# A hybrid decoder layer in TensorE's row: memory values in float32r, the norm of x placed earlier, eleven matmuls of ones ahead of the first product

## The chip, the core and the metric

The kernel runs on one core of one Trainium2 chip. The metric is the device time of one execution in microseconds (us), as a median over runs. A core has TensorE (PE in the profile, with its weight loads as PEld), VectorE (DVE), ScalarE (ACT), GpSimd (POOL) and SyncE (SP), which here only issues transfers. Each engine takes its instructions in the order in which they were written for it, and waits on semaphores for the others.

## The reference, cut to what matters

One decoder layer on x (1024 tokens of 1024 channels) with 256 memory tokens. The normalised input goes through one combined projection; three mixers use its columns (stick-breaking attention, an mLSTM, cross-attention to the memory tokens), their outputs are gated and merged, and a gated MLP with a short convolution follows. The change touches only the beginning, the norm of x and the keys and values of the memory:

```
h = _rmsnorm(x, g_mix[l])
(sb_q, sb_k, sb_v, ...) = jnp.split(h @ w_in[l], offsets, axis=-1)
...
y_xa = _memory_cross_attention(xa_q, _rmsnorm(mem, g_mem[l]), w_mem_kv[l], xa_g_q[l], xa_g_k[l])

def _memory_cross_attention(q, mem_n, w_kv, g_q, g_k):
    k, v = jnp.split(mem_n @ w_kv, 2, axis=-1)
```

## The kernel before, in words

Everything is stored transposed, channels on the 128 partitions and tokens along the free dimension, and x is handled in two halves of 512 tokens, half 1 first. A large product is made in float32r in three parts: an operand is split into a high piece (`hi`, an ACT copy that rounds to float32r) and a low piece (`lo`, a DVE subtraction of the high piece from the original), and `mm3` issues hi·hi, hi·lo and lo·hi into one PSUM bank. `split` (L135) and `wsplit` (L139) make these pieces. The memory's keys and values are the exception: `mem_mm` (L221) multiplies plain float32 tiles, one matmul per tile.

The first 60 us run like this. SP issues the vectors, the two halves of the memory (`y` tiles), the four key weights (`wk`), four pages of x's half 1, a small gate weight (`w_if`) and the four value weights (`wv`). ACT scales the memory by its gain (`mem_load`, L196). TensorE then makes the keys (`mem_mm` into the banks pk), 16 float32 matmuls of 128x512, and the values (into pv), another 16. Among them stand three small things: the norm factors of the memory (`mem_stats`: squares on ACT, adds on DVE, two matmuls with ones), those of x (`x_stats` and `rstd`: four squares on ACT, three adds on DVE, four matmuls with ones, a power on POOL), and `spread` (L172), which turns x's factors into rows by four DVE products with the identity and one matmul with ones. `x_norm` (L282) multiplies each of 8 channel tiles by gain and row factor on DVE (L287), and splits it into `h` tiles: hi on ACT, lo on DVE.

After the values comes the first projection, the queries and keys of the first attention pair (`chunks`, L389): two weights, `raw` tiles split into `whi` and `wlo`, times all 8 `h` tiles, 24 matmuls each, into two PSUM banks of the ring `pj`, which has two. `eq` and `ek` (L372 to L386) empty those banks with ACT copies and DVE subtractions. `gates_if` (L458) needs the first of them again for 16 matmuls, and `nat_chunks` (L348) the second. In that time the pages of x's half 0 arrive (L266), ACT squares them (L274), and the same norm is made for half 0.

Four things set the order around the change. The tiles of one tag are a ring with a fixed number of buffers (`raw`, `whi`, `wlo`: 2, `U`: 5, `pg`: 16), and the next user of a buffer waits until the last one is done. A scheduler places instructions by the order of the text and by priorities (`tc.high_priority`). Each engine then runs its row in that order. SP issues transfers in its own row too, so one that waits for a buffer holds back all behind it.

Of the kernel before, what the change touches and what calls it, by code (L numbers as in the profile page):

```python
# [11 lines left out]
F32R = mybir.dt.float32r  # L12
# [6 lines left out]
P = 128  # L19
D = 1024  # L20
S = 1024
HALF = 512
# [20 lines left out]
def tile_hybrid_layer(ctx: ExitStack, tc: tile.TileContext, xT, memT, vecs, w_t, w_n, w_kv, w_if,  # L43
# [58 lines left out]
    def hs(h):  # L102
        return slice(h * HALF, (h + 1) * HALF)
# [31 lines left out]
    def split(src, hi, lo, eng=None):  # L135
        nc.scalar.activation(hi, src, AF.Copy)  # L136
        (eng or nc.vector).tensor_sub(lo, src, hi.bitcast(F32))  # L137
# [48 lines left out]
    nc.scalar.activation(warm, nhalf[:, :1], AF.Square)  # L186
    mraw = []
    mg = [page() for _ in range(2)]

    def mem_load(j):  # L190
        t = T([P, S], "y")
        mraw.append(t)
        nc.sync.dma_start(t.rearrange("p (k m) -> p k m", k=4), memT[4 * j:4 * j + 4].rearrange("k p m -> p k m"))
        for i in range(4):
            c = slice(i * NMEM, (i + 1) * NMEM)
            nc.scalar.activation(mg[j][:, c], t[:, c], AF.Copy, scale=col(C_GMEM + 4 * j + i))  # L196

    mtags = itertools.cycle(("raw", "whi", "wlo"))

    def mem_w(which, b):  # L200
        t = T([P, S], next(mtags))
        nc.sync.dma_start(t, w_kv[which, b])
        return t

# [1 line left out]
    nc.vector.tensor_mul(gqk, col(C_GQ), col(C_GK))  # L206
    xkv_d = dtile([XAH, P, 2, NMEM], "xkv_d")

    def mem_stats():
        for t in mraw:  # L210
            nc.scalar.activation(t, t, AF.Square)
        a = mraw[0]
        nc.vector.tensor_add(a, a, mraw[1])
        for n in (512, 256):
            nc.vector.tensor_add(a[:, :n], a[:, :n], a[:, n:2 * n])
        pc = bank("tr")
        for t in range(2):
            nc.tensor.matmul(pc[:, t:t + 1], a[:, ts(t)], ones[:, :1], start=True, stop=True)
        return rstd_cols(pc[:, :2], 2, D)

    def mem_mm(pm, w, b):  # L221
        for m in range(2):
            for kk in range(2):
                k = 2 * b + kk
                c = slice((k % 4) * NMEM + m * P, (k % 4) * NMEM + (m + 1) * P)
                nc.tensor.matmul(pm[m], mg[k // 4][:, c], w[:, hs(kk)], start=(k == 0), stop=(k == KT - 1))  # L226

    def mem_keys(pm, rm):
        kns = []
# [62 lines left out]
    xp = {0: [], 1: []}  # L292
    wk, wv = [], []
    mem_load(0)
    wk.append(mem_w(0, 0))
    mem_load(1)
    for b in range(1, 4):
        wk.append(mem_w(0, b))
# [7 lines left out]
    for g in range(2):  # L306
# [1 line left out]
        hi = wif[:, :, 32 * g:32 * g + 4]  # L308
        nc.scalar.activation(hi, src, AF.Copy)
# [1100 lines left out]
```

## Time and profile before

| | |
|---|---|
| median of 3 runs | 1672.93 us (1672.88 to 1676.76) |
| the profiled execution's own time | 1674.48 us |
| its span in the trace | 1672.4 us |
| TensorE busy | 1645.0 us, 98% |
| DVE, ACT, POOL busy | 1209.2, 826.8, 52.8 us |
| first matmul starts | 6.91 us |
| first projection starts | 37.92 us |
| `gates_if` starts, `nat_chunks` starts | 49.96 us, 54.42 us |

A line of a timeline reads: start and length in us, engine, source line, operation, output and inputs, shape, count, and in square brackets the engine's idle time ahead of it with what ended it. Consecutive instructions of one kind are merged into a row with a count. TensorE's float32 matmul of 128x512 shows as two records, so a row of x8 is four matmuls. Records of matmuls overlap; what counts is the distance from one start to the next. SP's rows are issues, not transfers.

### The profile page before, as it was taken

What the parts mean: (1) busy time and instruction counts of PE and PEld (TensorE: products, weight loads), DVE (VectorE), ACT (ScalarE), POOL (GpSimd) and SP (SyncE); (2) the same over time, 40 slices, a digit from 0 to 9 for tenths busy, and PEclk for the clock granted to TensorE, in tenths of its full rate; (3) what the DMA queues carried; (4) which work ended last, traced back from release to release, by engine and by line L of the source; (5) the groups of instructions that cost most, each with busy time, mean ns of one, the idle gap of its engine ahead of it and who ended that gap; (6) DMA issues with size and microseconds to landing.
All of it is one profiled execution on the core that took longest, in us unless ns stands there. A gap on an engine that the chain in (4) does not pass through costs nothing.

```text
span 1672.4 us, 21192 instructions
## 1 busy us (share of the span) xinstructions
PE 1645.0 (98%) x7975; PEld 1338.0 (80%) x7975; DVE 1209.2 (72%) x1710; ACT 826.8 (49%) x1249; POOL 52.8 (3%) x95
## 2 busy tenths in 40 slices
PE   8999999999999999999999999999999999999999
PEld 4777777788877888888788888688888888788887
DVE  5648778777765666666557648997778877789864
ACT  4547667645555445556422334565455554543431
POOL 1000000010000001000000000000000000000000
PEclk9999999999999999999999999999999999999999
DMA  8410011234324555433755354222222221486131
GB/s 296 149 64 24 35 39 51 95 116 137 108 104 154 183 183 170 133 127 113 271 181 184 114 189 145 94 90 104 78 77 76 82 87 58 164 327 239 36 138 73
DMA packets 96249, 212.69 MB, mean 127 GB/s; under 512 B 12416, under 2 KB 36224, under 8 KB 96148
## 3 DMA queue, kind: packets, MB, share of 16 engines
q1 hardware_dynamic: 96148, 211.35, 37.1%
q8 instruction: 63, 1.03, 0.3%
q14 instruction: 38, 0.31, 0.1%
HBM read 156.71 MB, written 54.61 MB: 126 GB/s over the span
## 4 chain that ended last, share of the span: by engine, by line
PE 89%; DVE 4%; ACT 4%; DMA 3%; issue 1%; SPq 0%; POOLq 0%; POOL 0%; ACTq 0%; DVEq 0%
PE ps_pj L149 14%; PE ps_pj L150 14%; PE ps_pj L151 14%; PE ps_pv L150 6%; PE ps_pv L151 6%; PE ps_pv L149 6%; PE ps_tr L151 4%; PE ps_tr L149 4%; PE ps_tr L150 4%; PE ps_z L149 3%; PE ps_z L150 3%; PE ps_z L151 3%; PE ps_tr L434 2%; PE ps_pv L448 1%; PE ps_z L226 1%; PE ps_z L413 1%
## 5 line engine op out<-in xcount | busy, mean ns | idle before, releaser
L150 PE MATMUL ps_pj<-h,whi 128*128 128x512 f32 x620 | 242.2, 391 | 0.0
L136 ACT ACTIVATE whi<-raw 128x512 fp32r<-128x512 f32 (+1 forms) x112 | 93.6, 836 | 177.5 <-PE ps_pj L150 71.6
L149 PE MATMUL ps_pj<-h,whi 128*128 128x512 f32 x412 | 163.2, 396 | 0.9 <-DVE U L1053 0.9
L149 PE MATMUL ps_pj<-pg,whi 128*128 128x512 f32 x396 | 154.6, 390 | 0.0
L151 PE MATMUL ps_pj<-pg,wlo 128*128 128x512 f32 x380 | 148.0, 389 | 0.0
L150 PEld LDWEIGHTS ps_pj<-h,whi 128*128 128x128 f32 x620 | 116.5, 188 | 23.5 <-issue 0.2
L151 PE MATMUL ps_pj<-h,wlo 128*128 128x512 f32 x332 | 129.9, 391 | 0.1
L810 DVE SCALAR_TENSOR_TENSOR y<-U,vec,y 128x1023 f32<-128x1023 f32 x88 | 112.5, 1280 | 8.0 <-ACT y L808 8.0
L422 DVE TENSOR_TENSOR_SCAN U<-U 128x512 f32<-128x512 f32 (+3 forms) x96 | 88.6, 965 | 30.7 <-ACT U L415 29.8
L149 PEld LDWEIGHTS ps_pj<-h,whi 128*128 128x128 f32 x412 | 77.4, 188 | 18.3 <-issue 1.5
L137 DVE TENSOR_TENSOR wlo<-raw,whi 128x1024 fp32r<-128x1024 f32 x54 | 66.0, 1222 | 30.9 <-ACT whi L136 30.6
L149 PEld LDWEIGHTS ps_pj<-pg,whi 128*128 128x128 f32 x396 | 74.3, 188 | 15.8 <-DVE pg L1051 0.4
L151 PEld LDWEIGHTS ps_pj<-pg,wlo 128*128 128x128 f32 x380 | 71.3, 188 | 14.9 <-issue 0.2
L136 ACT ACTIVATE whi<-pg 128x512 fp32r<-128x512 f32 (+1 forms) x59 | 43.4, 738 | 72.2 <-PE ps_pv L150 20.7
L150 PE MATMUL ps_pj<-pg,whi 128*128 128x512 f32 x188 | 73.4, 390 | 0.0
L151 PEld LDWEIGHTS ps_pj<-h,wlo 128*128 128x128 f32 x332 | 62.3, 188 | 13.6 <-DVE wlo L137 0.6
L150 PE MATMUL ps_pv<-h,whi 128*128 128x512 f32 x164 | 63.8, 389 | 0.0
L808 ACT ACTIVATE y<-U,vec 128x1024 f32<-128x1024 f32 x44 | 54.6, 1241 | 14.7 <-DVE U L712 14.6
L151 PE MATMUL ps_pj<-h,whi 128*128 128x512 f32 x156 | 60.8, 390 | 0.0
L137 DVE TENSOR_TENSOR wlo<-raw,wlo 128x512 fp32r<-128x512 f32 x58 | 39.9, 688 | 23.0 <-ACT wlo L136 22.7
L151 PE MATMUL ps_tr<-pg,wlo 128*128 128x512 f32 x144 | 56.2, 390 | 0.1
L137 DVE TENSOR_TENSOR whi<-raw,whi 128x512 fp32r<-128x512 f32 x58 | 39.9, 688 | 22.0 <-ACT whi L136 22.0
(438 smaller groups left out, 4306.0 us busy)
## 6 DMA issues: line engine op xcount, KB each, us to landing
raw<-in_w_t_dram SPq DMA_DIRECT2D x29, 512.0 KB
gate_d<-U SPq DMA_DIRECT2D x24, 512.0 KB
U<-gate_d SPq DMA_DIRECT2D x24, 512.0 KB
pg<-in_w_up_dram SPq DMA_DIRECT2D x22, 512.0 KB
act_d<-y SPq DMA_DIRECT2D x22, 512.0 KB
pg<-in_w_t_dram SPq DMA_DIRECT2D x21, 512.0 KB
raw<-in_w_dn_dram SPq DMA_DIRECT2D x18, 512.0 KB
raw<-in_w_o_dram SPq DMA_DIRECT2D x16, 512.0 KB
```

What stands on the lines that cost most here:

```text
L136: nc.scalar.activation(hi, src, AF.Copy)
L137: (eng or nc.vector).tensor_sub(lo, src, hi.bitcast(F32))
L149: nc.tensor.matmul(out, lh, rh, start=start, stop=False, skip_group_check=more)
L150: nc.tensor.matmul(out, lh, rl, start=False, stop=False, skip_group_check=more)
L151: nc.tensor.matmul(out, ll, rh, start=False, stop=stop, skip_group_check=more)
L226: nc.tensor.matmul(pm[m], mg[k // 4][:, c], w[:, hs(kk)], start=(k == 0), stop=(k == KT - 1))
L413: nc.tensor.matmul(z[:, a, :w], qs[a][:, ts(rb)], kz[a][:, c], start=False, stop=True)
L422: nc.vector.tensor_tensor_scan(f[:, a, 1:w + 1], f[:, a, 1:w + 1], f[:, a, 1:w + 1], 1.0 if o == 0 else f[:, a, 0:1], op0=ALU.mult, op1=AL ...
L434: nc.tensor.transpose(pt[:, a, ts(j)], g[:, a, ts(j)], ident)
L448: nc.tensor.matmul(pv[64 * a:64 * a + 64, ts(rb % 4)], sbv[s // 2][:, s % 2, (2 * p + a) * 64:(2 * p + a + 1) * 64], wt[:, a, ts(j)], star ...
L808: nc.scalar.activation(out, u, AF.Identity, bias=bias, scale=taps[0])
L810: nc.vector.scalar_tensor_tensor(out[:, :S - s], u[:, s:], taps[s], out[:, :S - s], op0=ALU.mult, op1=ALU.add)
```

## The change

Eleven float32 matmuls of the 128x128 ones with themselves are put in front of the first product, into a bank that nothing else uses then. Both halves of the scaled memory are split into hi and lo (`mgr`, four pages of the ring `pg`), right behind the scaling. The four value weights are split too, and the values are made with `mem_mm3`: 48 float32r matmuls in place of 16 float32 ones. The value weights land in other buffers: two in the ring `U`, two in `raw`. In SP's row the fourth key weight and `w_if` now stand ahead of the pages of x. The squares of the memory are added up behind the values in the text (`mem_squares`, the sum kept in an `me` tile), and the two matmuls with ones on them (`mem_rstd`) come late, among the chunks of `nat_chunks`. The norm of x stands earlier in TensorE's row: its four matmuls with ones after five of the 48 value matmuls, and `spread` after fifteen. The second half of the value weights is split at a high priority.

Behind the transposes of the memory's keys, in the first 100 us of the trace before, the rows of all engines are the same as before. Lines of the changed kernel have higher numbers: 4 more for `split` and `mm3`, 24 or 25 more from `sb_qk` on.

```diff
+    first = bank("tr")
+    for _ in range(11):
+        nc.tensor.matmul(first[:, :P], ones, ones, start=True, stop=True)
...
+    mgr = [[page(dt=F32R) for _ in range(2)] for _ in range(2)]
...
             nc.scalar.activation(mg[j][:, c], t[:, c], AF.Copy, scale=col(C_GMEM + 4 * j + i))
+        split(mg[j], *mgr[j])
-    def mem_stats():
+    def mem_squares():
         for t in mraw:
             nc.scalar.activation(t, t, AF.Square)
-        a = mraw[0]
-        nc.vector.tensor_add(a, a, mraw[1])
-        for n in (512, 256):
-            nc.vector.tensor_add(a[:, :n], a[:, :n], a[:, n:2 * n])
+        a, b = mraw
+        out = T([P, HALF], "me")[:, :NMEM]
+        nc.vector.tensor_add(a, a, b)
+        nc.vector.tensor_add(a[:, :HALF], a[:, :HALF], a[:, HALF:])
+        nc.vector.tensor_add(out, a[:, :NMEM], a[:, NMEM:HALF])
+        return out
+
+    def mem_rstd(a):
         pc = bank("tr")
...
+    def mem_mm3(pm, w, b, ms=(0, 1)):
+        for m in ms:
+            for kk in range(2):
+                k = 2 * b + kk
+                c = slice((k % 4) * NMEM + m * P, (k % 4) * NMEM + (m + 1) * P)
+                mm3(pm[m], mgr[k // 4][0][:, c], mgr[k // 4][1][:, c], w[0][:, hs(kk)], w[1][:, hs(kk)],
+                    k == 0, k == KT - 1)
...
-    mem_mm(pk, wk[0], 0)
-    mem_mm(pk, wk[1], 1)
-    rm = mem_stats()
-    mem_mm(pk, wk[2], 2)
-    mem_mm(pk, wk[3], 3)
-    for b in range(4):
-        wv.append(mem_w(1, b))
-    r = rstd(x_stats(xp[1]), HALF)
-    mem_mm(pv, wv[0], 0)
-    x_norm(1, xp[1], spread(r, 4))
-    for b in range(1, 4):
-        mem_mm(pv, wv[b], b)
+    for b in range(3):
+        mem_mm(pk, wk[b], b)
+    wraws = [mem_w(1, 0, "U")]
+    a = x_stats(xp[1])
+    wraws += [mem_w(1, b, ("raw", "raw", "U")[b - 1]) for b in range(1, 4)]
+    mem_mm(pk, wk[3], 3, (0,))
+    r = rstd(a, HALF)
+    mem_mm(pk, wk[3], 3, (1,))
+    wv.append(wsplit(None, raw=wraws[0]))
+    mem_mm3(pv, wv[0], 0, (0,))
+    rows = spread(r, 4)
+    wv.append(wsplit(None, raw=wraws[1]))
+    x_norm(1, xp[1], rows)
+    mem_mm3(pv, wv[0], 0, (1,))
+    mem_mm3(pv, wv[1], 1)
+    for b in range(2, 4):
+        with tc.high_priority(offset=200):
+            wv.append(wsplit(None, raw=wraws[b]))
+        mem_mm3(pv, wv[b], b)
+    squares = mem_squares()
...
     for _ in range(3):
         next(vals)
+    rm = mem_rstd(squares)
     kn = mem_keys(pk, rm)
```

Three places in the rows of the engines show what the text alone does not.

ScalarE, from the scaling of the memory on, before (`pg_96`, `pg_97`: the scaled memory; the four `U` tiles: squares of x; `pg_151`: the gate weight `w_if`):

```order
L196 ACTIVATE pg_96<-y_121,vec 128x256 x4
L211 ACTIVATE y_121<-y_121 128x1024
L196 ACTIVATE pg_97<-y_129,vec 128x256 x4
L211 ACTIVATE y_129<-y_129 128x1024
L274 ACTIVATE U_193<-pg_137 128x1024
L274 ACTIVATE U_195<-pg_139 128x1024
L274 ACTIVATE U_198<-pg_143 128x1024
L274 ACTIVATE U_201<-pg_145 128x1024
L309 ACTIVATE pg_151<-hf_149 128x8x4 x2
```

The same place now (`pg_171`: `w_if`; `U_189` and `whi_221`: the first value weight and its hi piece):

```order
L201 ACTIVATE pg_108<-y_137,vec 128x256 x4
L140 ACTIVATE pg_110<-pg_108 128x1024
L215 ACTIVATE y_137<-y_137 128x1024
L201 ACTIVATE pg_109<-y_147,vec 128x256 x4
L140 ACTIVATE pg_112<-pg_109 128x1024
L215 ACTIVATE y_147<-y_147 128x1024
L325 ACTIVATE pg_171<-hf_169 128x8x4 x2
L290 ACTIVATE U_191<-pg_157 128x1024
L290 ACTIVATE U_193<-pg_159 128x1024
L290 ACTIVATE U_196<-pg_163 128x1024
L290 ACTIVATE U_199<-pg_165 128x1024
L140 ACTIVATE whi_221<-U_189 128x1024
```

Two hi copies have come in, the copies of `w_if` have moved from behind the squares of x to in front of them, and the hi piece of the first value weight follows the squares. The copies of `w_if` write a page that DVE clears first (L305, now L321), and in DVE's row that clearing stands behind the lo piece of the second memory half and the three adds of the memory's squares.

TensorE at the end of the values and the start of the first projection, before (`ps_pj_306`: queries; `whi_302`, `wlo_303`: pieces of their weight; `h_101` and on: hi, `h_109` and on: lo pieces of x):

```order
L226 MATMUL ps_pv_119<-whi_191,pg_97 128x512 x2
L226 MATMUL ps_pv_120<-whi_191,pg_97 128x512 x2
L149 MATMUL ps_pj_306<-h_101,whi_302 128x512
L150 MATMUL ps_pj_306<-h_109,whi_302 128x512
L151 MATMUL ps_pj_306<-h_101,wlo_303 128x512
L149 MATMUL ps_pj_306<-h_102,whi_302 128x512
```

The same place now (`ps_pj_368`: queries, `ps_pj_403`: keys; `whi_364`, `wlo_365` and `whi_399`: their weights' pieces):

```order
L154 MATMUL ps_pv_136<-wlo_309,pg_112 128x512
L155 MATMUL ps_pv_136<-whi_308,pg_113 128x512
L153 MATMUL ps_pj_368<-h_117,whi_364 128x512
L154 MATMUL ps_pj_368<-h_125,whi_364 128x512
L153 MATMUL ps_pj_403<-h_117,whi_399 128x512
L154 MATMUL ps_pj_403<-h_125,whi_399 128x512
L155 MATMUL ps_pj_368<-h_117,wlo_365 128x512
L153 MATMUL ps_pj_368<-h_118,whi_364 128x512
```

Two matmuls of the second product now stand ahead of the first one's third matmul, which is the first to read `wlo_365`. DVE's row around that lo piece, before:

```order
L137 TENSOR_TENSOR h_109<-U_224,h_101 128x512
L287 SCALAR_TENSOR_TENSOR U_232<-pg_139,vec,ps_tr_222 128x512
L137 TENSOR_TENSOR h_110<-U_224,h_102 128x512
L137 TENSOR_TENSOR wlo_303<-raw_300,whi_302 128x1024
L137 TENSOR_TENSOR h_111<-U_232,h_103 128x512
```

and now:

```order
L303 SCALAR_TENSOR_TENSOR U_266<-pg_165,vec,ps_tr_236 128x512
L141 TENSOR_TENSOR h_131<-U_266,h_123 128x512
L141 TENSOR_TENSOR wlo_365<-raw_362,whi_364 128x1024
L141 TENSOR_TENSOR h_132<-U_266,h_124 128x512
L141 TENSOR_TENSOR wlo_400<-raw_397,whi_399 128x1024
```

Before, the lo piece of the first projection's weight came after two of the eight lo pieces of x. Now it comes after seven of them.

SP at the same place, before (`hn_d`: store of the normalised x; `raw_335`: the second projection weight; `raw_399`, `raw_405`: weights of `nat_chunks`; `pg_292` to `pg_298`: x's half 0):

```order
L289 DMA hn_d<-U_232 128x1024
L142 DMA raw_335<-in_w_t_dram 128x1024
L142 DMA raw_399<-in_w_n_dram 128x1024
L289 DMA hn_d<-U_240 128x1024
L289 DMA hn_d<-U_248 128x1024
L266 DMA pg_292<-in_xT_dram 128x2x512
L266 DMA pg_294<-in_xT_dram 128x2x512
L266 DMA pg_296<-in_xT_dram 128x2x512
L266 DMA pg_298<-in_xT_dram 128x2x512
L142 DMA raw_405<-in_w_n_dram 128x1024
```

and now (`raw_461`, `raw_467`: the weights of `nat_chunks`; `pg_354` to `pg_360`: x's half 0):

```order
L305 DMA hn_d<-U_250 128x1024
L305 DMA hn_d<-U_258 128x1024
L305 DMA hn_d<-U_266 128x1024
L146 DMA raw_461<-in_w_n_dram 128x1024
L146 DMA raw_467<-in_w_n_dram 128x1024
L282 DMA pg_354<-in_xT_dram 128x2x512
L282 DMA pg_356<-in_xT_dram 128x2x512
L282 DMA pg_358<-in_xT_dram 128x2x512
L282 DMA pg_360<-in_xT_dram 128x2x512
```

Both weights now stand ahead of the pages. Each reuses a `raw` buffer, and waits until DVE has made the lo piece of the weight in it: `raw_461` for `wlo_365`, `raw_467` for `wlo_400`.

More of the change, by code (lines that the diff above doesn't have):

```diff
@@ L196, in mem_load, with mem_w @@
             nc.scalar.activation(mg[j][:, c], t[:, c], AF.Copy, scale=col(C_GMEM + 4 * j + i))
-    mtags = itertools.cycle(("raw", "whi", "wlo"))
-    def mem_w(which, b):
-        t = T([P, S], next(mtags))
+        split(mg[j], *mgr[j])
+    def mem_w(which, b, tag):
+        t = T([P, S], tag)
         nc.sync.dma_start(t, w_kv[which, b])
@@ L219, in mem_stats, with mem_mm @@
         return rstd_cols(pc[:, :2], 2, D)
-    def mem_mm(pm, w, b):
-        for m in range(2):
+    def mem_mm(pm, w, b, ms=(0, 1)):
+        for m in ms:
             for kk in range(2):
@@ L226, in mem_mm @@
                 nc.tensor.matmul(pm[m], mg[k // 4][:, c], w[:, hs(kk)], start=(k == 0), stop=(k == KT - 1))
+    def mem_mm3(pm, w, b, ms=(0, 1)):
+        for m in ms:
+            for kk in range(2):
[3 more added lines that the diff above has]
+                    k == 0, k == KT - 1)
     def mem_keys(pm, rm):
@@ L294, in tile_hybrid_layer @@
     mem_load(0)
-    wk.append(mem_w(0, 0))
+    wk.append(mem_w(0, 0, "raw"))
     mem_load(1)
     for b in range(1, 4):
-        wk.append(mem_w(0, b))
+        wk.append(mem_w(0, b, ("raw", "whi", "wlo")[b - 1]))
         if b < 3:
```

## The prediction

> **What bounds the kernel now.** I read the page first.
>
> ```profile
> PE 1645.0 (98%) x7975; PEld 1338.0 (80%) x7975; DVE 1209.2 (72%) x1710; ACT 826.8 (49%) x1249; POOL 52.8 (3%) x95
> ```
>
> TensorE is busy for 98% of the span, so a stage gets shorter only where TensorE gets less work or waits less, and any new wait of TensorE is paid in full. Next come TensorE's waits (engine, tile and line, released by whom: us in total, times, longest).
>
> ```profile
> PE ps_z L226 <- ACT pg L196: 6.9, 1, 6.9
> ...
> PE ps_pj L462 <- DVE pg L377: 0.6, 1, 0.6
> PE ps_pj L149 <- DVE pg L386: 0.5, 1, 0.5
> ```
>
> In the part that changes it waits 6.9 us for the first product, then not until `gates_if` (L462) and `nat_chunks` (L149), where both banks of `pj` are still being emptied. These two waits are short, but they show that the emptying has no slack. The third view is TensorE's timeline.
>
> ```profile
> 6.91 5.34 PE L226 MATMUL ps_z<-raw,pg 128*128 128x512 f32 x8 [6.91 <-ACT pg L196]
> 12.09 3.60 PE L226 MATMUL ps_z<-whi,pg 128*128 128x512 f32 x8
> 15.52 0.50 PE L218 MATMUL ps_tr<-ones,y 128*128 128x1 f32 x4
> ...
> 27.16 1.02 PE L179 MATMUL ps_tr<-hf,ones 128*128 128x512 f32 x2
> ...
> 31.45 3.60 PE L226 MATMUL ps_pv<-raw,pg 128*128 128x512 f32 x8
> 34.89 3.60 PE L226 MATMUL ps_pv<-whi,pg 128*128 128x512 f32 x8
> 37.92 0.79 PE L149 MATMUL ps_pj<-h,whi 128*128 128x512 f32 x1
> 39.01 0.40 PE L149 MATMUL ps_pj<-h,whi 128*128 128x512 f32 x1
> 39.70 0.40 PE L149 MATMUL ps_pj<-h,whi 128*128 128x512 f32 x1
> ...
> 49.96 0.45 PE L462 MATMUL ps_pj<-h,pg 128*100 128x512 f32 x1 [0.55 <-DVE pg L377]
> ...
> 54.42 0.47 PE L149 MATMUL ps_pj<-pg,h 128*128 128x512 f32 x1 [0.53 <-DVE pg L386]
> ```
>
> Four float32 matmuls take 34.89 - 31.45 = 3.44 us, 0.86 each; three float32r ones 39.70 - 39.01 = 0.69, 0.23 each. The first eight records take 5.34 us where later ones take 3.60.
>
> **The savings on TensorE.** 16 x 0.86 = 13.8 us of values become 48 x 0.23 = 11.0: 2.7 less. The eleven matmuls run while TensorE would wait anyway (6.9 us), so they cost nothing; if they bring the later rate to the first four products they save 5.34 - 3.60 = 1.74, and otherwise nothing. At most the change gains 4.5 us, which is 0.27%.
>
> [...]
>
> **The price on ACT and DVE.** The new pieces need six more full-page hi copies on ACT and six lo pieces on DVE ahead of the first projection. ACT's timeline:
>
> ```profile
> 5.56 1.70 ACT L196 ACTIVATE pg<-y,vec 128x256 f32<-128x256 f32 x4 [3.33 <-DMA y<-in_memT_dram]
> 7.29 1.06 ACT L211 ACTIVATE y<-y 128x1024 f32<-128x1024 f32 x1
> 8.40 1.70 ACT L196 ACTIVATE pg<-y,vec 128x256 f32<-128x256 f32 x4
> ...
> 12.90 1.06 ACT L274 ACTIVATE U<-pg 128x1024 f32<-128x1024 f32 x1 [1.71 <-DMA pg<-in_xT_dram]
> ...
> 16.94 1.06 ACT L274 ACTIVATE U<-pg 128x1024 f32<-128x1024 f32 x1 [0.30 <-DMA pg<-in_xT_dram]
> 18.46 0.35 ACT L309 ACTIVATE pg<-hf 128x32 fp32r<-128x32 f32 x2 [0.47 <-DMA hf<-in_w_if_dram]
> ...
> 38.52 1.06 ACT L136 ACTIVATE whi<-raw 128x1024 fp32r<-128x1024 f32 x1 [0.79 <-PE ps_pv L226]
> ```
>
> DVE's timeline:
>
> ```profile
> 11.22 1.23 DVE L213 TENSOR_TENSOR y<-y,y 128x1024 f32<-128x1024 f32 x1 [7.31 <-ACT y L211]
> ...
> 13.79 0.91 DVE L305 MEMSET pg<- 128x1024 f32 x1 [0.16 <-issue]
> ...
> 16.67 2.58 DVE L277 TENSOR_TENSOR U<-U,U 128x1024 f32<-128x1024 f32 x2
> ...
> 23.82 0.16 DVE L155 TENSOR_SCALAR sm<-ps_tr 128x4 f32<-128x4 f32 x1 [3.64 <-PE ps_tr L165]
> 25.11 0.88 DVE L177 TENSOR_SCALAR hf<-ident,sm 128x128 f32<-128x128 f32 x4 [1.13 <-POOL sm L157]
> 28.22 2.06 DVE L287 SCALAR_TENSOR_TENSOR U<-pg,vec,ps_tr 128x512 f32<-128x512 f32 x3 [2.23 <-PE ps_tr L179]
> ...
> 32.07 1.22 DVE L137 TENSOR_TENSOR wlo<-raw,whi 128x1024 fp32r<-128x1024 f32 x1
> 33.20 0.68 DVE L137 TENSOR_TENSOR h<-U,h 128x512 fp32r<-128x512 f32 x1
> 33.81 0.74 DVE L287 SCALAR_TENSOR_TENSOR U<-pg,vec,ps_tr 128x512 f32<-128x512 f32 x1
> 34.46 0.68 DVE L137 TENSOR_TENSOR h<-U,h 128x512 fp32r<-128x512 f32 x1
> ```
>
> Packed, DVE makes a full-page lo piece in 1.13 (32.07 to 33.20), a half-page one in 0.61, an L287 product in 0.65. The times below are places on the span's clock.
>
> 1. ACT scales from 5.56 to 7.3, then copy 8.4, square 9.4, scaling 11.1, copy 12.2. DVE makes the second memory lo until 13.4; the squares' adds and the clearing took 11.22 to 14.70, 3.48, so they end at 16.9. Now the copies of `w_if` wait for that and hold the squares of x behind them: 0.35 to 17.25. The pages of x are in time: one 512 KB transfer (16.94 - 12.90 over three, 1.35) is ahead of them now, so they land at 14.25 to 18.3.
> 2. Four squares (1.0 each packed) end at 21.3, the hi of the first value weight at 22.3. TensorE is through the keys at 6.9 + 13.8 = 20.7 and waits. If the first product stays slow it is through at 22.4: the warm-up is worth nothing here.
> 3. DVE's three adds (1.29 each) start after the second square, 19.3 to 23.2; first value lo 24.3; last add 25.0; second lo 26.15. TensorE's matmuls with ones end about then. From L155 to the identity products 25.11 - 23.82 = 1.29, 27.45; they take 0.88, 28.3; the `spread` matmul 28.22 - 27.16 = 1.06 plus about 0.4 of loading, 29.8. The third value lo fits in that wait. So `x_norm` starts at 29.8, against 28.22: in time the norm of x is not earlier.
> 4. Then DVE's row has 8 products, 7 half-page lo pieces, the fourth value lo and `wlo_365`: 5.2 + 4.3 + 2.3 = 11.8, and about 0.3 of waiting for the fourth hi, whose buffer TensorE must free. The lo piece ends at 41.9.
> 5. TensorE needs 11.0 us for the values, after 22.3 some 3 us of waits, 1.0 for `spread` and about as much for the four matmuls with ones: it is through at 37 to 38, does the four matmuls that need no lo piece, and stands still until 41.9. Its second `h` tile comes at 42.1 against 39.01, with two matmuls (0.46) done in advance: 2.7 us later. Both savings are gone.
>
> **The pages of half 0.** SP, ACT and DVE after that:
>
> ```profile
> 1.18 0.42 SPq L193 DMA_DIRECT2D y<-in_memT_dram  x1
> ...
> 38.73 2.41 SPq L266 DMA_DIRECT2D pg<-in_xT_dram  x4
> ...
> 46.24 1.06 ACT L274 ACTIVATE U<-pg 128x1024 f32<-128x1024 f32 x1 [1.36 <-DMA pg<-in_xT_dram]
> ...
> 47.80 0.59 ACT L375 ACTIVATE pg<-ps_pj 64x512 fp32r<-64x512 f32 x1
> 48.42 2.01 ACT L274 ACTIVATE U<-pg 128x1024 f32<-128x1024 f32 x2
> 50.45 0.59 ACT L381 ACTIVATE pg<-ps_pj 64x512 fp32r<-64x512 f32 x1
> ...
> 52.26 0.59 ACT L384 ACTIVATE pg<-ps_pj 64x512 fp32r<-64x512 f32 x1
> ...
> 52.89 0.68 DVE L385 TENSOR_TENSOR pg<-ps_pj,pg 64x512 fp32r<-64x512 f32 x1
> ```
>
> 6. The pages' issues stand behind `raw_467`, which waits for `wlo_400`: 41.9 + 0.61 + 1.13 = 43.7, against 38.73. How long they take to land is open. The first page before took 46.24 - 38.73 = 7.5, with stores ahead of it; the memory's first half, with an empty queue, landed 5.56 after the start of the span, 4.4 after its issue (1.18). I take 5.3: two weights of 1.35 are ahead and already under way. The first page lands at 49.0; the ends are 48 and 51.2.
> 7. ACT's row then has the square of that page, the hi of `raw_461` (51.0) and only then the two copies that empty the first `pj` bank. From the second copy's start to `gates_if` 49.96 - 47.80 = 2.16: 51.6 + 2.16 = 53.8. TensorE, with 46 matmuls left at 41.9, would be ready at 52.5.
> 8. `gates_if` takes 54.42 - 0.53 - 49.96 = 3.9, to 57.7. The second bank: copies end at 52.2, three squares 55.2, a hi copy 56.2, four copies (52.85 - 50.45 = 2.4) 58.6, then 54.42 - 52.89 = 1.5 to TensorE: 60.1. So `nat_chunks` starts at 60.1 against 54.42: 5.7 later. The two matmuls of the memory's norm (0.50) stood before that point and now come after it: 6.2 in all.
>
> Later the rows are the same and TensorE's waits hang on its own products, so the delay stays. The memory's factors, now late, are covered: 41 matmuls (9.4 us) lie between them and the transposes of the keys, and on the way stand two steps like the one from L155 to L177 (1.29 each) and short instructions on ACT and DVE.
>
> The profiled execution would go from its own time of 1674.48 to 1680.7. It lies 1.6 above the median of the runs, which I take as the base: 1672.9 + 6.2 = 1679.1.
>
> **The rivals.** A measurement of this kernel can tell about 0.3%, 5.0 us, from no change.
>
> - The pages land in time for ACT, or the squares of x do not wait. Then TensorE pays step 5, and the second bank alone: first product through at 47.2, second at 52.5, `gates_if` to 56.4, copies and subtractions of the second bank 52.5 + 2.4 + 1.5 = 56.4. That is 2.0 + 0.5 = 2.5 later, 1675.4. For it: the landing is my least known number. Against: the issue cannot come before `wlo_400`. [...]
> - The other side, a gain: DVE and ACT hide their work and TensorE never waits. It gives 1672.9 - 4.5 = 1668.4. It holds from the point where `wlo_365` is done by about 34, eight us before step 4 has it. The rows leave no room for that; the savings themselves are sure.
> - The pages take 7.5 us as before: two us more in steps 6 to 8, 1681.3.
> - The change does not do what it says: in time the norm comes no earlier (step 3). That is part of the forecast.
>
> **How the numbers follow.** Forecast 0.56 (1678 to 1680.5), pages early 0.24, pages slow 0.16, gain 0.04. The forecast and the slow pages are mostly beyond 5.0 us, so slower by over 0.3% has 0.67; the early pages and the gain lie within, with some of the forecast: 0.30; faster by over 0.3% would need more than both savings: 0.03. The range, 1674.0 to 1682.5, leaves out the gain, the shortest of the early cases, and slow pages with a later lo piece.
>
> **What would show it.** Right: TensorE waits on DVE's `wlo` for over 2 us ahead of the first projection's third matmul, near 42; the first square of half 0 starts near 49; `gates_if` and `nat_chunks` wait on L401 and L410, the latter starting near 60. Wrong: no such wait, or `nat_chunks` starting before 57; then a link of steps 1 to 6 is shorter than its row before, or a later stage takes the delay back.

## The result, and the profile after

Over six runs each, the changed kernel takes 1682.63 us (1680.36 to 1685.73) where the kernel before takes 1673.57: 9.06 more, a ratio of 1.0052 with a 95% interval of 1.0039 to 1.0064. It is slower. The profiled execution took 1681.51, with a span of 1679.7 against 1672.4.

The page gives the busy times of the engines over the span.

```profile
PE 1652.5 (98%) x8013; PEld 1350.0 (80%) x8013; DVE 1217.3 (72%) x1716; ACT 831.9 (50%) x1255; POOL 52.4 (3%) x95
```

TensorE is busy 7.5 us longer than before (1645.0). The eleven matmuls, about 5, stand against savings of 2.7 on the values and 1.4 on the keys; so waits are not the whole of the loss, and some matmuls also take longer. TensorE's waits after (engine, tile and line, released by whom: us in total, times, longest) name the first part.

```profile
PE ps_pj L155 <- DVE wlo L141: 3.1, 1, 3.1
PE ps_pj L486 <- DVE pg L401: 2.0, 1, 2.0
...
PE ps_pv L154 <- DVE wlo L141: 1.5, 1, 1.5
...
PE ps_pj L153 <- DVE pg L410: 0.8, 1, 0.8
```

Before, only the two waits at `gates_if` and `nat_chunks` were there, 0.6 and 0.5. TensorE's timeline places them (line numbers are those of each kernel's own file; `gates_if` is L486 here, `nat_chunks` starts with the L153 at 64.29).

```profile
6.18 7.50 PE L234 MATMUL ps_z<-raw,pg 128*128 128x512 f32 x16
...
21.16 0.73 PE L153 MATMUL ps_pv<-whi,pg 128*128 128x512 f32 x2 [0.60 <-ACT whi L140]
23.37 0.50 PE L154 MATMUL ps_pv<-wlo,pg 128*128 128x512 f32 x1 [1.49 <-DVE wlo L141]
...
28.53 0.63 PE L155 MATMUL ps_pv<-whi,pg 128*128 128x512 f32 x1
28.96 0.63 PE L153 MATMUL ps_pv<-whi,pg 128*128 128x512 f32 x1
...
30.24 1.35 PE L183 MATMUL ps_tr<-hf,ones 128*128 128x512 f32 x2
31.65 0.40 PE L154 MATMUL ps_pv<-wlo,pg 128*128 128x512 f32 x1
31.89 0.40 PE L155 MATMUL ps_pv<-whi,pg 128*128 128x512 f32 x1
...
44.17 0.50 PE L155 MATMUL ps_pj<-h,wlo 128*128 128x512 f32 x1 [3.13 <-DVE wlo L141]
58.01 0.56 PE L486 MATMUL ps_pj<-h,pg 128*100 128x512 f32 x1 [1.97 <-DVE pg L401]
64.29 0.47 PE L153 MATMUL ps_pj<-pg,h 128*128 128x512 f32 x1 [0.79 <-DVE pg L410]
```

The warm-up works: sixteen records of key matmuls (eight matmuls) take 7.50, where the first sixteen took 8.94 before (5.34 + 3.60). Before, the records start 0.85 apart up to 9.60 and 0.43 apart from 10.80 on; now 0.43 apart from 7.09 on. TensorE then stands still three times on the way to the first projection. `gates_if` starts 8.05 later than before (58.01 against 49.96), `nat_chunks` 9.87 (64.29 against 54.42).

The windows view explains the longer matmuls (stretch, its length, busy time of each engine with its instructions, then PEclk, the clock that TensorE was granted as a share of full speed, the DMA share, GB/s):

```profile
20.90:24.30 3.40, 1.66 (x6) 1.05 (x7) 3.34 (x4) 1.26 (x2) 0.00 (x0) 0.96 0.97 374
24.30:31.10 6.80, 6.80 (x22) 5.41 (x20) 2.61 (x7) 1.91 (x2) 1.03 (x1) 0.52 0.36 127
31.20:38.00 6.80, 6.80 (x30) 5.45 (x29) 6.13 (x10) 4.26 (x6) 0.00 (x0) 1.00 0.39 154
...
44.80:48.20 3.40, 3.40 (x10) 2.61 (x10) 3.32 (x3) 0.00 (x0) 0.00 (x0) 0.54 0.71 202
...
58.40:61.80 3.40, 3.40 (x10) 2.35 (x9) 3.30 (x4) 3.35 (x5) 0.00 (x0) 0.53 0.20 75
```

Three stretches have TensorE at half clock, each right after one of the waits. In this trace the clock changes at 24.06 and 30.89, 44.54 and 47.95, 58.19 and 61.61: the stretches are 6.83, 3.41 and 3.41 long, and begin 20.48 and 13.65 apart, 6 and 4 times 3.41. So it changes here only at borders of windows of 3.41 us. Together the stretches last 13.6 us, so by an estimate up to 6.8 us of work are lost in them; that is about the 6.5 by which TensorE's busy time grew beyond the eleven matmuls less the two savings. In the profile before there is no such stretch between the first product and the end. In the first of the three a float32r matmul starts every 0.43 us (28.53 to 28.96 in the timeline above) instead of every 0.24 (31.65 to 31.89), and the `spread` matmul, which stands behind ten of them in TensorE's row, starts at 30.24.

The other engines at the places that the prediction names: ACT's, SP's and DVE's rows.

```profile
16.02 0.35 ACT L325 ACTIVATE pg<-hf 128x32 fp32r<-128x32 f32 x2 [3.74 <-DVE pg L321]
...
53.18 1.06 ACT L290 ACTIVATE U<-pg 128x1024 f32<-128x1024 f32 x1 [9.19 <-DMA pg<-in_xT_dram]
...
55.09 0.57 ACT L398 ACTIVATE pg<-ps_pj 64x512 fp32r<-64x512 f32 x1
```

```profile
44.19 2.06 SPq L146 DMA_DIRECT2D raw<-in_w_n_dram  x2
46.31 2.36 SPq L282 DMA_DIRECT2D pg<-in_xT_dram  x4
```

```profile
42.89 1.23 DVE L141 TENSOR_TENSOR wlo<-raw,whi 128x1024 fp32r<-128x1024 f32 x1
```

ACT is idle for 9.19 us before the first square of half 0. The page was issued at 46.31, behind two raw weights, and they behind the lo piece that DVE made at 42.89 as one of the last of its row.

What became of the delay is read by matching each ACT and DVE instruction with the same one in the profile before, and taking the median difference of their start times over a stretch (us on the clock of before). The second profile of each kernel is from an experiment below.

```
stretch       changed  changed again  before again
 90 to 110     10.83       12.45         -0.47
200 to 230     11.05       12.68         -0.41
640 to 680      9.98       12.91         -0.92
700 to 740      8.61       11.62         -0.94
1000 to 1040    7.69       10.72         -1.50
1065 to 1100    7.68       10.72         -0.05
1650 to 1690    7.35       10.38          0.20
```

Nearly all of the loss is made before 200 us (the second profile adds 0.4 up to 400 us). Of the delay at 200 us, 3.7 are given back by the end of the first profile, 2.3 by the end of the second.

### The profile page after: what moved, and what is told of

It reads as the page before. It is cut to its first block, busy times and chain, and to the rows that moved or that the text cites. A ratio compares the mean times of both kernels' runs of the same rounds, so it can differ in the third digit from the quotient of the medians.

```text
span 1679.7 us, 21289 instructions
## 1 busy us (share of the span) xinstructions
PE 1652.5 (98%) x8013; PEld 1350.0 (80%) x8013; DVE 1217.3 (72%) x1716; ACT 831.9 (50%) x1255; POOL 52.4 (3%) x95
## 4 chain that ended last, share of the span: by engine, by line
PE 87%; DVE 4%; ACT 4%; DMA 2%; issue 1%; POOL 0%; POOLq 0%; SPq 0%; DVEq 0%; ACTq 0%
PE ps_pj L153 14%; PE ps_pj L154 13%; PE ps_pj L155 13%; PE ps_pv L154 6%; PE ps_pv L155 6%; PE ps_pv L153 6%; PE ps_tr L153 4%; PE ps_tr L155 4%; PE ps_tr L154 4%; PE ps_z L153 3%; PE ps_z L155 3%; PE ps_z L154 3%; PE ps_tr L458 1%; PE ps_pv L472 1%; DMA raw<-y_d 1%
## 5 line engine op out<-in xcount | busy, mean ns | idle before, releaser
L153 PE MATMUL ps_pj<-h,whi 128*128 128x512 f32 x412 | 163.6, 397 | 0.9 <-ACT whi L140 0.7
L153 PE MATMUL ps_pj<-pg,whi 128*128 128x512 f32 x396 | 154.7, 391 | 0.2 <-DVE pg L1076 0.2
L446 DVE TENSOR_TENSOR_SCAN U<-U 128x512 f32<-128x512 f32 (+3 forms) x96 | 88.6, 965 | 30.6 <-ACT U L439 29.7
L153 PEld LDWEIGHTS ps_pj<-h,whi 128*128 128x128 f32 x412 | 77.8, 189 | 18.0 <-ACT whi L140 1.2
L153 PEld LDWEIGHTS ps_pj<-pg,whi 128*128 128x128 f32 x396 | 74.4, 188 | 16.0 <-DVE pg L1076 0.7
```

Of the source, the lines that this page charges most:

```text
L153: nc.tensor.matmul(out, lh, rh, start=start, stop=False, skip_group_check=more)
L446: nc.vector.tensor_tensor_scan(f[:, a, 1:w + 1], f[:, a, 1:w + 1], f[:, a, 1:w + 1], 1.0 if o == 0 else f[:, a, 0:1], op0=ALU.mult, op1=AL ...
```

## The experiments

**One part out: the values back in float32** (`f32_values`). The six added hi and lo pieces go; the eleven matmuls, the earlier norm in the text, the order of the loads and the later norm of the memory stay.

```
-        split(mg[j], *mgr[j])
...
-    wv.append(wsplit(None, raw=wraws[0]))
-    mem_mm3(pv, wv[0], 0, (0,))
+    mem_mm(pv, wraws[0], 0, (0,))
...
-    mem_mm3(pv, wv[0], 0, (1,))
-    mem_mm3(pv, wv[1], 1)
...
+    mem_mm(pv, wraws[0], 0, (1,))
+    for b in range(1, 4):
+        mem_mm(pv, wraws[b], b)
```

> The changed kernel with the values back in float32 from unsplit weights and unsplit memory pages (16 float32 matmuls, none of the six added hi and lo pieces); the eleven matmuls of the ones, the earlier norm in the text, the order of the loads and the later norm of the memory stay. By my theory the added pieces cause all three waits (3.13 ahead of the first projection's third matmul, 1.97 at gates_if, 0.79 at nat_chunks) and the two of 0.60 and 1.49 in the values: none over 1 is left between 7 and 65, the granted clock stays full, nat_chunks starts at 52.5 to 54.5, and the time is that of before or up to 1.7 less: 1671.8 to 1673.8, ratio to before 0.999 to 1.000. Rival (the moves by themselves cost: the order of SP's row, the later norm of the memory): 1677 or more.

1675.55 us over eleven runs against 1674.85: ratio 1.0002 (0.9993 to 1.0010). Its TensorE timeline:

```profile
6.66 7.11 PE L232 MATMUL ps_z<-raw,pg 128*128 128x512 f32 x16 [1.35 <-ACT pg L200]
...
17.95 3.67 PE L232 MATMUL ps_z<-wlo,pg 128*128 128x512 f32 x8 [0.75 <-DMA wlo<-in_w_kv_dram]
...
49.59 0.45 PE L479 MATMUL ps_pj<-h,pg 128*100 128x512 f32 x1 [0.69 <-DVE pg L394]
54.05 0.47 PE L153 MATMUL ps_pj<-pg,h 128*128 128x512 f32 x1 [0.52 <-DVE pg L403]
```

The two waits at `pj` are those of before, `nat_chunks` starts at 54.05, and the profiled execution's mean granted clock is 1.000. The whole loss hangs on the split pieces. The moves cost nothing that can be measured, and the warm-up with the moves wins nothing: the first 1.8 saved (8.94 to 7.11) goes into a wait for a weight's DMA and into the same emptying of `pj`.

**One part alone: the eleven matmuls in the kernel before** (`warm_only`).

```
+    first = bank("tr")
+    for _ in range(11):
+        nc.tensor.matmul(first[:, :P], ones, ones, start=True, stop=True)
```

> The kernel before with nothing but the eleven matmuls of the ones. In the changed kernel the first sixteen matmuls of the keys took 7.50 where they took 8.94 before, so 1.4 to 1.7 are saved at the start. My theory: the saving is not kept whole, since gates_if waits for the emptying of the first bank of pj, which hangs on ACT's row and on the pages of half 0, and these come earlier only as far as their buffers are freed earlier; the wait of 0.55 at gates_if grows to 1 to 2, and the time is 0.3 to 1.2 under that of before, ratio 0.9993 to 0.9998. Rival (TensorE's work alone counts): the whole 1.7, ratio 0.9990. Second rival (the matmuls cost something elsewhere, or the windows of the clock fall differently): no gain, 1.000 or above.

1674.09 over eleven runs against 1674.73: ratio 1.0001 (0.9992 to 1.0010). The gain is not there, neither the whole of it nor the part that I expected; 0.9993 is still inside the interval. The timeline shows where the saving went:

```profile
6.14 3.67 PE L229 MATMUL ps_z<-raw,pg 128*128 128x512 f32 x8 [0.68 <-ACT pg L199]
10.43 3.67 PE L229 MATMUL ps_z<-whi,pg 128*128 128x512 f32 x8 [0.62 <-DMA whi<-in_w_kv_dram]
...
19.00 3.67 PE L229 MATMUL ps_z<-raw,pg 128*128 128x512 f32 x8 [0.69 <-DMA raw<-in_w_kv_dram]
...
50.90 0.45 PE L465 MATMUL ps_pj<-h,pg 128*100 128x512 f32 x1 [1.82 <-DVE pg L380]
```

TensorE is now ahead of its weights and waits for two of them, and the wait at `gates_if` has grown from 0.55 to 1.82. The edit is small, but the scheduler also placed other instructions differently. SP's row, and then ACT's:

```profile
41.28 2.31 SPq L269 DMA_DIRECT2D pg<-in_xT_dram  x4
```

```profile
50.32 1.04 ACT L139 ACTIVATE whi<-raw 128x1024 fp32r<-128x1024 f32 x1
```

The pages of half 0 now go out behind a raw weight (40.89), 2.55 later than before (38.73), where that weight stood behind them. And ACT makes the next weight's hi piece ahead of the four copies that empty the second bank, which start at 51.38; before, they started at 50.45, with the hi piece behind them at 53.71. So this run does not test the warm-up with all else equal: what it would win in the rows of before stays open.

With the pages of half 0 issued by GpSimd's queue as well (`warm_only_pp`):

> The kernel before with the eleven matmuls of the ones and with the four pages of half 0 of x issued from GpSimd's queue instead of SP's, where they stood behind stores of the norm (38.73 in the profile before). By my theory the pages land 1.5 to 3 earlier, ACT reaches the emptying of the first bank earlier, and the saving at the start is kept: gates_if near 48.2 to 49 instead of 49.96, nat_chunks near 52.5 to 53.5 instead of 54.42, the time 1.0 to 2.2 under that of before, ratio 0.9987 to 0.9994. Rival (the emptying hangs on the hi piece of the next weight in ACT's row, not on the pages): as with the eleven matmuls alone.

Ratio 0.9999 (0.9990 to 1.0008). The wait at `gates_if` is gone, but `nat_chunks` starts where it did, and waits longer:

```profile
54.51 0.47 PE L152 MATMUL ps_pj<-pg,h 128*128 128x512 f32 x1 [1.25 <-DVE pg L389]
```

The pages were only one of two things that the emptying of the second bank hangs on. The other is that hi piece: ACT makes it at 49.45, ahead of the four copies still, and they start at 50.53, no earlier than in the kernel before.

**The change without the eleven matmuls** (`no_warm`): the diff above, with minus signs and without the line of `first`.

> The changed kernel without the eleven matmuls of the ones; the rows of the other engines are as in it. First theory (the new pieces in ACT's and DVE's rows decide, TensorE's clock does not): the first product is back at half clock and its matmuls end about 1.7 later (5.34 against 3.60 for the first eight before), near 22.3 instead of 20.6; but the third matmul of the values waits for DVE's first lo piece at 23.37 either way, so from there on nothing moves: 1682.6, within 1 of the changed kernel. Second theory (the clock): in the changed kernel the two waits of 0.60 and 1.49, which fall into one stretch of 3.4 us, are followed by 6.8 us at half clock (24.3 to 31.1), and that makes the spread of the norm 1.8 late. Without the eleven matmuls those waits shrink to about 1.0 or less, the clock stays, the first product of the norm starts near 30 instead of 31.62, and all that follows is up to 1.8 earlier: 1680.8 to 1681.5.

1683.60 over five runs: ratio 1.0054 (1.0041 to 1.0066), as the changed kernel. The timeline, though, has moved as the second theory said:

```profile
23.82 0.50 PE L152 MATMUL ps_pv<-wlo,pg 128*128 128x512 f32 x1 [1.48 <-DVE wlo L139]
...
28.02 1.10 PE L181 MATMUL ps_tr<-hf,ones 128*128 128x512 f32 x2
...
55.40 0.45 PE L484 MATMUL ps_pj<-h,pg 128*100 128x512 f32 x1 [1.01 <-DVE pg L399]
61.68 0.47 PE L151 MATMUL ps_pj<-pg,h 128*128 128x512 f32 x1 [2.34 <-DVE pg L408]
```

Only the wait of 1.48 is left, and in this execution it falls, by an estimate, across the border of two windows (the next stretch at half clock begins at 40.3; if the borders stand 3.41 apart here too, one lies 5 x 3.41 before it, at 23.2). TensorE was busy for 2.54 and 2.78 of the 3.4 us on its two sides. The clock stays full up to there, and the `spread` matmul starts 2.2 earlier (28.02 against 30.24) though DVE's first lo piece is 0.45 later. `nat_chunks` is 2.6 earlier. By the table's measure the lead is 3.0 at 90 us, but 1.6 at 400 (8.81 against 10.38), and later it is gone: another stretch at half clock at 1057.5 costs 1.35, and less is given back near 690 (0.5, against 1.4). So the clock is shown to move the early stage; that it moves the time these two kernels don't show. Their times differ by less than their intervals can tell.

The executions of one kernel, each with its mean granted clock on record, say more. The changed kernel took 1680.36 and 1681.73 at 0.997, 1681.51 and 1683.53 at 0.996, 1684.92 and 1685.73 at 0.995. The medians of `late_pool`, below, are 1675.67 at 0.999, 1678.14 at 0.998 and 1679.60 at 0.997. One window of 3.41 us at half clock takes 0.001 off the mean of such a span (1.7 of 1680). So time and clock go together within a kernel, by some 1.5 to 2.8 us for each 0.001 in these medians and means, though not everywhere: the five executions of `no_warm` all had 0.997 and lie 3.1 apart. It is not shown which comes first, since a longer wait lengthens the time, and the stretches at half clock came after waits.

**The first projection's lo piece earlier in DVE's row** (`lo_first`). A higher priority for the splits in the loop that makes the first attention pair, so for both of its weights (queries and keys); the pieces of the norm's last pages come after them.

```
-        with tc.high_priority(offset=SOON):
+        with tc.high_priority(offset=soon[0]):
...
+    soon[0] = 120
...
+    soon[0] = SOON
```

> The changed kernel with a higher priority for the split of the first projection's weight, so that its lo piece stands some six pieces earlier in DVE's row (ahead of the products and lo pieces of the last pages of the norm). By my theory the wait of 3.13 ahead of the third matmul of the first projection (44.17) goes: under 0.5 is left. But in ACT's row the hi pieces of the next two weights then stand ahead of the emptying of the first bank, and the first of them needs a buffer that TensorE frees only with its last matmul of the projection: two hi pieces and a square of 1.0 each and 2.16 from the first copy to TensorE give a wait of about 5 at gates_if instead of 1.97. Net: nat_chunks 2.5 to 4 earlier than 64.29, time 1678.5 to 1680.5. Rival (the pages of half 0 or the clock set the end, not this lo piece): the wait at gates_if grows by as much as the other shrinks, 1682.6.

1678.33 over eleven runs: ratio 1.0021 (1.0012 to 1.0030). The wait of 3.13 is gone and one takes its place:

```profile
52.60 0.72 PE L487 MATMUL ps_pj<-h,pg 128*100 128x512 f32 x1 [5.45 <-DVE pg L402]
```

This was forecast (about 5), with its reason: two hi pieces stand ahead of the emptying in ACT's row, and the first needs a buffer that TensorE frees at the end of the projection. ACT's row has them at 46.33, `x2`, 2.00 long. Over half of the loss is back, but not by the lo piece alone. The raw weights are now issued from 36.23 and the pages from 41.64 (44.19 and 46.31 in the changed kernel), and in this profile no stretch at half clock follows the first waits (1.00 from 19.7 to 26.5): `x_norm` starts at 29.21 instead of 31.62, which the two moved pieces, both later in DVE's row, do not explain.

**The pages of half 0 from GpSimd's queue** (`pool_pages`). Every other row is as in the changed kernel.

```
-    def x_page(h, i):
+    def x_page(h, i, eng=nc.sync):
...
-    xp[0] = [x_page(0, i) for i in range(4)]
+    xp[0] = [x_page(0, i, nc.gpsimd) for i in range(4)]
```

> The changed kernel with the four pages of half 0 of x issued from GpSimd's queue instead of SP's; every other row is as in it. By my theory they are late because they stand behind the second raw weight in SP's row, which waits for a lo piece (issues at 44.19 and 46.31). From GpSimd they can go when TensorE is through with the values, near 39.5, and land 5 to 7 later: first square of half 0 near 46 instead of 53.18. ACT's row then waits for the raw weight of the next product (issued at 44.19, landing near 50 to 52) and empties the bank of the first projection near 52.5 to 54: gates_if 1 to 2 earlier than 58.01, nat_chunks 1 to 2.5 earlier than 64.29, time 1680.1 to 1681.6. Rival: the pages are not the link, the raw weight or TensorE itself is, and with the queue shared the raw weight lands later by what the pages take: no gain, 1682.6 or a little more.

1679.78 over eleven runs: ratio 1.0026 (1.0017 to 1.0035), a little better than expected. GpSimd's queue, ACT and TensorE:

```profile
33.58 2.17 POOL L282 DMA_DIRECT2D pg<-in_xT_dram  x3 [4.92 <-PE ps_pv L155]
```

```profile
50.63 1.06 ACT L140 ACTIVATE whi<-raw 128x1024 fp32r<-128x1024 f32 x1 [5.87 <-PE ps_pj L154]
```

```profile
43.99 0.79 PE L155 MATMUL ps_pj<-h,wlo 128*128 128x512 f32 x1 [3.13 <-DVE wlo L141]
60.80 0.47 PE L153 MATMUL ps_pj<-pg,h 128*128 128x512 f32 x1 [1.42 <-DVE pg L410]
```

The pages go out over 12 us earlier, ACT no longer waits for them, and `nat_chunks` starts 3.5 earlier, with the wait for the lo piece as it was. So SP's row is a link of its own, as step 6 had it.

**Two value lo pieces on GpSimd** (`late_pool`): the third and fourth split with `eng=nc.gpsimd`.

> The changed kernel with the lo pieces of the third and fourth value weight made by GpSimd instead of VectorE; their later place lets ACT empty the first bank ahead of one square more. DVE's row ahead of the first projection's lo piece is two pieces of 1.13 shorter. By my theory (DVE's row decides) the wait of 3.13 ahead of the third matmul shrinks to 0.5 to 1.0, gates_if and nat_chunks come 2 to 4 earlier than 58.01 and 64.29, and the time is 1676.5 to 1680. How long GpSimd takes for such a piece no trace shows; if it takes over about 4, TensorE waits for it in the values instead and nothing is won. Rival (TensorE's clock decides): the first two waits (0.60 and 1.49) stay, so the stretch at half clock near 24 to 31 stays too where both fall into one window, and the gain is under 1.

1678.08 over eleven runs: ratio 1.0021 (1.0011 to 1.0030).

```profile
30.26 2.38 POOL L141 TENSOR_TENSOR wlo<-raw,whi 128x1024 fp32r<-128x1024 f32 x1 [2.98 <-ACT whi L140]
```

```profile
42.94 0.50 PE L155 MATMUL ps_pj<-h,wlo 128*128 128x512 f32 x1 [0.71 <-DVE wlo L141]
54.97 0.45 PE L486 MATMUL ps_pj<-h,pg 128*100 128x512 f32 x1 [1.75 <-DVE pg L401]
```

The wait of 3.13 shrinks to 0.71: DVE's row did set it. The first stretch at half clock is there as before (24.7 to 31.5), with `spread` at 30.17; the two later ones, which followed the longer waits, are gone with them. At 200 us the delay is 5.97 instead of 11.05. The four executions at a granted clock of 0.999 took 1675.20 to 1676.08, where those of the kernel before at the same clock have a median of 1675.35: what is left of the loss here goes together with the clock.

**Both at once** (`late_pool_pp`), and the same without the eleven matmuls (`late_pool_pp_nw`):

> The changed kernel with two of its links relieved at once: the lo pieces of the third and fourth value weight on GpSimd (2.38 us each there), and the four pages of half 0 of x from GpSimd's queue, behind those two pieces (the second ended at 37.42). With the pieces alone the square of the first page waited 2.10 for the page (51.26) and gates_if 1.75 for the emptying behind it (54.97). By my theory (a chain of links in DVE's, SP's and ACT's rows) the pages now land before 49, gates_if starts 1 to 1.75 earlier, at 53.2 to 54, nat_chunks near 57.5 to 58.4 instead of 59.43, and the time is 1 to 2 under the one with the pieces alone (ratio 1.0021): ratio 1.0010 to 1.0016. Rival (the pages only push the next raw weight back on the same engines): no gain, 1.0021 or above.

> As the kernel of the same call, without the eleven matmuls of the ones; every other row is the same. By the theory of the clock the first product then ends 1.7 later, the waits of 0.69 and 1.48 in one window of 3.4 us shrink to 1.5 or less, the stretch at half clock that follows goes away or moves, the spread of the norm starts 1.5 to 2.2 earlier (28.0 in the changed kernel without these matmuls against 30.24 with them), and the places up to nat_chunks come up to 2 earlier than with them: nat_chunks near 55.5 to 57. The time is up to 2 lower, ratio 1.0000 to 1.0012, as far as no later wait is then followed by half clock. Rival (the clock does not matter for the end): nat_chunks and the time as with the eleven matmuls, or later by up to 1.7.

Ratios 1.0025 (1.0016 to 1.0035) and 1.0032 (1.0020 to 1.0044): neither is better than one relief alone, and my expectation failed twice. ACT's timeline of the first, and TensorE's of the second:

```profile
50.27 1.06 ACT L140 ACTIVATE whi<-raw 128x1024 fp32r<-128x1024 f32 x1 [7.57 <-DMA raw<-in_w_n_dram]
```

```profile
23.60 0.50 PE L152 MATMUL ps_pv<-wlo,pg 128*128 128x512 f32 x1 [0.79 <-DVE wlo L139]
...
27.78 1.10 PE L181 MATMUL ps_tr<-hf,ones 128*128 128x512 f32 x2
...
53.96 0.45 PE L484 MATMUL ps_pj<-h,pg 128*100 128x512 f32 x1 [3.59 <-DVE pg L399]
```

Now the raw weight of the next product is what ACT waits for, 7.57. It was issued at 41.75 and is there at 50.27, 8.5 later; in `late_pool`, with the pages behind it, it was issued at 42.96 and there by 48.09, at most 5.1 later. So the pages' head start pushes it back, as the recorded rival had it. Without the eleven matmuls the clock is full up to 55 and `spread` starts at 27.78 instead of 29.48, but `gates_if` waits 2.3 longer (3.59 against 1.30), since the raw weight still comes late. At 90 us the lead is 0.3, and the time is not lower. Here the clock's cost was hidden behind the DMA.

**Both kernels once more, one profile each** (`after_again`, `before_again`).

> The changed kernel once more, one profile. The instructions and their rows are the same. By the theory of the clock the windows of 3.41 us lie elsewhere on the span, so the first two waits (0.60 and 1.49) may fall into one window or into two: if into two, no stretch at half clock follows them and the spread of the norm starts near 28 to 28.5 instead of 30.24; the wait of 3.13 stays, and nat_chunks starts 0 to 2.5 earlier than 64.29. Later, the wait of 1.7 near 1050 may be followed by half clock here, where it was not in the first profile. If the clock follows the kernel's work alone and not the windows, the stretches stand at the same places (24.3, 44.8, 58.4) within 0.5.

> The kernel before once more, one profile. Up to nat_chunks it has no wait over 1 after the first product, so no window is idle enough, the clock stays full, and nat_chunks starts within 0.5 of 54.42. Near 1050 the wait of 1.7 stands; by the theory of the windows it is followed by 3.4 at half clock, or not, as the windows fall; the first profile had none.

One run each, 1684.54 and 1674.53. The changed kernel has its stretches at half clock at 23.8 to 30.6, 44.3 to 47.7 and 64.8 to 68.2: the third followed `nat_chunks`' wait, now 2.34, and not `gates_if`'s. The kernel before shows one late in the span, after a wait of 1.7 that it also had in its first profile. Here are that place in the two profiles of before, and a stretch with a wait of 1.82 in the kernel with the eleven matmuls alone; the first row of each pair has the wait, the second is what follows.

```profile
1044.80:1048.20 3.40, 1.68 (x8) 1.05 (x6) 3.40 (x6) 1.92 (x3) 0.00 (x0) 1.00 0.01 2
1048.20:1051.60 3.40, 2.83 (x12) 1.81 (x11) 3.40 (x4) 1.66 (x2) 0.00 (x0) 1.00 0.00 0
```

```profile
1045.70:1049.10 3.40, 2.25 (x7) 1.33 (x8) 3.40 (x5) 2.54 (x3) 0.00 (x0) 0.97 0.00 0
1049.10:1052.50 3.40, 3.40 (x10) 2.65 (x9) 3.40 (x5) 1.06 (x1) 0.00 (x0) 0.53 0.00 0
```

```profile
49.20:52.60 3.40, 1.70 (x8) 1.26 (x9) 3.19 (x4) 3.33 (x6) 0.00 (x0) 1.00 0.65 249
52.70:56.10 3.40, 2.88 (x13) 1.87 (x12) 2.68 (x4) 3.39 (x5) 0.00 (x0) 1.00 0.42 154
```

The same kernel with the same wait kept its clock once and lost it once, at a price of 1.45 (the table's third column, -1.50 to -0.05). So the stretches belong to the execution, not to the kernel alone.

## Why the prediction was right, and where its sizes were off

The direction and the mechanism held: DVE's row of split pieces makes the first projection's lo piece late, SP's row holds the pages behind it, ACT's row the emptying behind these, and both of TensorE's savings are lost on the way. `f32_values` shows that the pieces are the cause; `late_pool`, `lo_first` and `pool_pages` show the links, each worth about half of the loss. `lo_first` moved the pages and met another clock as well, so the cleaner evidence is the other two. Forecast 6.2 more, measured 9.06. The median, 1682.63, lies 0.13 above the upper end of the range, 1682.5; the base had moved too, from 1672.9 to 1673.57, and the measured ratio on the forecast's base gives 1681.6, near that end. By the prediction's steps:

1. Held, about 1 early: the copies of `w_if` at 16.02 (forecast to end at 17.25), after a 3.74 wait for the clearing.
2. Held: first value product at 21.16 (22.3).
3. **This step failed in size.** The first lo piece came early (TensorE at 23.37), the identity products started at 27.38 (27.45). But the `spread` result was forecast for 29.8 and `x_norm` started at 31.62: 1.8 late, since the ten value matmuls ahead of the `spread` matmul ran at half clock.
4. DVE's stretch from there was sized right: 31.62 to 44.12 is 12.5, forecast 11.8 and 0.3. The lo piece ended at 44.12 instead of 41.9; 1.8 of the 2.2 are step 3's.
5. "Stands still until 41.9": 3.13, at 44.17.
6. **The landing was undersized.** Issue at 46.31, forecast 43.7; the first page was 6.87 on its way (53.18 - 46.31), where I took 5.3 between 4.4 and 7.5. Of the 4.2 that the first square is late, 2.6 are the issue and 1.6 the landing. `pool_pages` bears out the queue; how much the raw weights ahead add to a landing was not measured apart.
7. `gates_if` at 58.01, forecast 53.8: the 4.2 of step 6, no more (55.68 to 58.01 is 2.33, 2.16 before).
8. `nat_chunks` at 64.29, forecast 60.1: again 4.2. The moved norm of the memory was not quite covered: a wait of 0.3 at the transposes of the keys comes to its 0.5.

"So the delay stays" was wrong in the other direction: 11.05 at 200 us became 7.35 at the end of the first profile, 12.68 became 10.38 in the second. The largest single step is 1.3 to 1.4 near 690, where both profiles of before have a wait of 1.3 that neither of the changed kernel has. The two errors partly cancel in the sum; that the first profiled execution, 7.0 longer than the one before, comes so near to 6.2 is luck. The forecast's sum has no term for a drop of the clock within the kernel. Step 3 shows 1.8 of it, and the six executions of the changed kernel, 5.4 apart, lie nearly in the order of their clocks.

The rivals: a gain needed the lo piece by 34, and it was ten later. Early pages did not happen. The slow pages (1681.3) are nearest to what was measured, with the clock added. In the changed kernel's first profile half clock followed waits as short as 0.60 and 1.49 close together, and one of 1.97 alone. The stretches are 3.4 or 6.8 long, and lie elsewhere in each execution of one kernel (by the windows view 24.3, 44.8 and 58.4 in the first profile, 23.8, 44.3 and 64.8 in the second). That the clock column reads 1.00 at the slow start of the kernel before, where the records stand 0.85 apart in place of 0.43, means little: its trace has no record of the clock ahead of 10.28 us, where full clock begins, and the column counts what has no record as full.

No version here beats the kernel before. `f32_values`, `warm_only` and `warm_only_pp` can't be told from it.

## What to carry to other kernels

Splitting an operand for cheaper matmuls moves work onto the engines that feed TensorE: before counting the matmuls saved, add up the row of the feeding engine to the first piece that TensorE needs next. When one link of such a chain is relieved, look at once for the next one (here the lo piece, the pages, the raw weight): two reliefs together, 1.0025, gave no more than one, 1.0021 or 1.0026. Compare the rows of all engines after an edit, even one that only adds instructions, since the scheduler may have moved others with it. And a short wait can be dearer than it looks: here 6.8 us at half clock followed two of 0.60 and 1.49, and with them `x_norm` started 1.8 later than forecast.

## What the hardware showed

- TensorE's stretches at half clock (0.51 to 0.54 in the column) lasted 3.4 or 6.8 us. In the windows looked at, under 1.5 us of busy time of 3.4 was followed by half clock each time (0.15 to 1.43, nine windows in six profiles); between 1.55 and 2.25 both happened (1.55, 1.65, 1.68 and 1.70 kept it; 1.66, 1.91, 1.92, 1.92 and 2.25 did not). The stretches were placed to about 0.3 us; what decides within that band, these runs don't settle.
- One such window near 1050 us put what follows 1.4 us later, by the measure of the table above (the kernel before again 1.45, at 1049.1; `no_warm` 1.35, at 1057.5). An early one did not show in the time where another link ended later anyway: `late_pool_pp` had one at 25.9 and a wait of ACT of 7.57 for a raw weight behind it, and its time, 1679.53, is not above the 1681.34 of the same kernel without the eleven matmuls, whose clock was full there (1.00 from 24.4 to 27.8).
- GpSimd took 2.38 us for a 128x1024 lo piece (`late_pool`), DVE 1.13 from one start to the next (32.07 to 33.20 in the kernel before).
